# The end of a one-layer mixer and MoE kernel: residual rows summed by TensorE, second rows added by accumulating DMAs, VectorE's order written out

## The chip, the cores and the metric

The kernel runs on one core of a Trainium2 chip. The metric is device time in microseconds of one execution; of several runs the median is taken. Besides these runs one execution was recorded by the hardware profiler; all durations and starts below are from that one, in microseconds from the start of its span unless marked ns.

## The reference

One layer of a diffusion backbone over 512 latent tokens of width 1024 (and 256 context tokens, which feed only the mixer). Behind the mixer and its residual comes a mixture of experts, then one more residual and a last norm:

```python
gates = jnp.sum(jax.nn.one_hot(expert_id, N_EXPERTS, dtype=jnp.float32) * top_w[..., None], axis=1).astype(t.dtype)
y = jnp.zeros_like(t)
for e in range(N_EXPERTS):
    a = jax.nn.silu(t @ w_gate[e]) * (t @ w_up[e])
    y = y + gates[:, e:e + 1] * (a @ w_down[e])
...
xs = xs + g2x * hierarchical_moe(modulate(rms_norm(xs, norm2_w[l]), sh2x, sc2x), *moe_args)
...
return rms_norm(xs, final_norm_w)
```

Each token goes to 2 of 16 experts. `g2x` is a row of 1024 factors, the same for all tokens; `rms_norm` divides a row by the root of its mean square (plus 1e-6) and multiplies it by a row of weights. All of it is float32.

## The kernel before

The last third of the kernel works expert by expert, up to 128 tokens each. The tokens of an expert are gathered from DRAM (`xg`), transposed by TensorE, multiplied by the gate and up weights (`pg`, `pu`, line 1524), gated (`a`), transposed again (`at`, line 1542), multiplied by the down weights (`py`, line 1555). To keep float32 accuracy each factor is split in a high and a low part (`hi`, `lo`, `ah`, `al`), and a product is three products of 512 columns in a faster type. The result `y`, weighted, is scattered by GpSimd's DMA to rows of `y_d` in DRAM (line 1389). Each token has two rows there, next to each other, one for each of its experts.

The last expert (15) does not go through DRAM. Its y is multiplied by g2 as well (line 1559), split into `yh` and `yl` (lines 1585 and 1586), and brought to the token rows by products with a one-hot matrix `oht` (lines 1594 and 1595, accumulators `pz{t}{j}`: tile t, half j). The 512 tokens are four tiles t of 128. For each, the other experts' rows are loaded from `y_d` (`yv`, both rows of a token, 1 MB, line 1576, issued by SP), the two rows are added by GpSimd (line 1577), multiplied by g2 (`g2b`, line 1578) and added to the residual `xs1` (line 1579), VectorE both. Then VectorE adds the accumulators to `xs1` (line 1596). The end of a tile is the norm: ScalarE squares and sums (line 1599), VectorE makes the mean (line 1600), GpSimd raises it to -1/2 (line 1601), VectorE multiplies by it and by the final weights `fw` (line 1602), and the tile `o` is stored, by SP's queue for even t and ScalarE's for odd (line 1603). `o` has two buffers for four tiles.

The order of the instructions on each engine is decided when the program is built, by a scheduler that simulates them; it is not the order of the code where nothing forces it. `tc.add_manual_dep(b, a, behind)` forces b behind a on one engine without a semaphore; `put` does so for TensorE, behind the product that was put before. `psA` and `psB` take accumulators of one bank from pools: two for `psA` (which `py` uses), six for `psB`. `raw_tile` takes the tiles of yv from the weights' buffers.

Of the kernel before, what the change touches and what calls it, by code (L numbers as in the profile page):

```python
# [16 lines left out]
P = 128  # L17
# [203 lines left out]
def tile_kernel(ctx, tc, x, c, ctxt, c_ctx, w_mod, b_mod, norm1_w, norm2_w, w_in, w_out, hg_lb, hg_norm_w,  # L221
# [1278 lines left out]
    for t in range(NLT):  # L1500
        nc.vector.tensor_scalar(oht[:, t, :], K("iota"), 128.0 * t, tl, op0=ALU.add, op1=ALU.is_equal)

    def up(e, before):
# [34 lines left out]

    def down(e, a):
        pt = psB(f"at{e}")  # L1540
        for k in range(4):
            nc.tensor.transpose(pt[:, k * P:(k + 1) * P], a[:, k * P:(k + 1) * P], ident)  # L1542
        ah = mw2.tile([P, 4, P], F32R, tag="ah", name=f"ah{e}", bufs=2)
        al = mw2.tile([P, 4, P], F32R, tag="al", name=f"al{e}", bufs=2)
        pv = pt.rearrange("p (k t) -> p k t", k=4)
        nc.scalar.copy(ah, pv)  # L1546
        nc.vector.tensor_sub(al, pv, ah.bitcast(F32))  # L1547
        y = mw2.tile([P, D], F32, tag="y", name=f"y{e}", bufs=2)
        for j in range(2):
# [81 lines left out]
```

## Time and profile before

| | |
|---|---|
| median of 3 runs | 970.18 us (967.68 to 970.53) |
| the profiled execution | 971.5 us, span 969.7 us |
| TensorE busy | 879.4 us, 91% of the span, granted clock 0.964 on the mean |
| VectorE busy | 732.4 us, 76% |
| ScalarE, GpSimd busy | 500.8 us, 217.8 us |
| loads of `y_d` into yv | 4, of 1 MB each |

The span runs from the first to the last instruction; the execution's time has some 1.8 us around it. Busy time is an average over stages with different limits, so the shares say little about the last 30 us, in which the change lies. A line such as L1577 in a row is a line of the kernel; names of tiles stand as out<-in. A granted clock of 1.00 is TensorE's upper level, 2.4 GHz; 0.50 is 1.2 GHz.

### The profile page before, as it was taken

How to read it: one execution, taken by the hardware profiler on the slowest of the kernel's cores; microseconds unless marked ns; L12 is line 12 of the kernel's file. 1: busy time of each engine (PE TensorE's matmuls, PEld its weight loads, DVE VectorE, ACT ScalarE, POOL GpSimd, SP SyncE). 2: the span in 40 equal slices, each digit the busy share in tenths (PEclk: the TensorE clock that was granted, in tenths of full speed). 3: DMA queues.
4: the chain of work that ended last, by engine and by line, in shares of the span. 5: the costliest groups of instructions: out<-in, count | busy, mean ns of one | idle time of the engine just before them, and what ended most of it. 6: DMA issues, size and time to landing. Idle time of an engine off the chain costs nothing. (4 is left out here: it accounts for less than half of the span.)

```text
span 969.7 us, 20466 instructions
## 1 busy us (share of the span) xinstructions
PE 879.4 (91%) x8205; PEld 720.3 (74%) x8205; DVE 732.4 (76%) x1378; ACT 500.8 (52%) x958; POOL 217.8 (22%) x225
## 2 busy tenths in 40 slices
PE   3999998989989999899999989899999999999962
PEld 1678877878768887787886868758888887777741
DVE  2598589746799579964474656768899898888887
ACT  4345532454246344432432333138888887887832
POOL 2232631251135213411111110011111110110040
PEclk9999998999979999899998999999999999999995
DMA  9920350201102111047227288579999999999442
GB/s 307 313 66 13 110 205 24 69 21 35 35 23 55 35 33 47 12 144 233 63 86 255 64 269 312 181 253 387 380 363 367 366 362 378 369 377 364 176 186 87
DMA packets 115436, 180.03 MB, mean 186 GB/s; under 512 B 9863, under 2 KB 49347, under 8 KB 114824
## 3 DMA queue, kind: packets, MB, share of 16 engines
q1 hardware_dynamic: 108536, 164.28, 49.8%
q0 software_dynamic: 6048, 13.13, 3.7%
q8 instruction: 66, 1.08, 0.5%
q10 hardware_dynamic: 752, 1.25, 0.4%
q14 instruction: 34, 0.28, 0.1%
HBM read 170.31 MB, written 16.27 MB: 192 GB/s over the span
## 5 line engine op out<-in xcount | busy, mean ns | idle before, releaser
L1409 DVE TENSOR_TENSOR lo<-w,hi 128x1024 fp32r<-128x1024 f32 x184 | 216.7, 1221 | 26.6 <-ACT hi L1404 24.9
L1404 ACT CAST hi<-w 128x1024 fp32r<-128x1024 f32 x184 | 186.0, 1050 | 21.7 <-PE pu L1524 9.7
L1555 PE MATMUL py<-lo,ah 128*128 128x512 f32 x128 | 51.6, 403 | 0.8
L1555 PE MATMUL py<-hi,ah 128*128 128x512 f32 x128 | 50.5, 395 | 0.7 <-ACT ah L1546 0.7
L1555 PE MATMUL py<-hi,al 128*128 128x512 f32 x128 | 49.4, 396 | 0.3 <-DVE al L1547 0.3
L1524 PE MATMUL pg<-lo,xh 128*128 128x512 f32 x120 | 48.6, 405 | 0.0
L1524 PE MATMUL pu<-lo,xh 128*128 128x512 f32 x120 | 48.2, 401 | 0.2 <-DVE lo L1409 0.2
L1524 PE MATMUL pu<-hi,xh 128*128 128x512 f32 x120 | 47.6, 396 | 0.0
L1524 PE MATMUL pg<-hi,xh 128*128 128x512 f32 x120 | 47.5, 396 | 0.0
L1389 POOL DMA_INDIRECT y_d<-y,cl x15 | 17.6, 1174 | 132.9 <-ACT y L1557 119.7
L1524 PE MATMUL pu<-hi,xl 128*128 128x512 f32 x120 | 47.3, 394 | 0.0
L1524 PE MATMUL pg<-hi,xl 128*128 128x512 f32 x120 | 47.3, 394 | 0.0
L815 POOL TENSOR_TENSOR am<-atr,cst 128x128 f32<-128x128 f32 x32 | 17.8, 558 | 123.1 <-PE po L818 108.2
L1382 POOL DMA_INDIRECT xg<-t_d,cl x15 | 19.5, 1303 | 114.3 <-PE xt L1512 104.5
L938 DVE TENSOR_TENSOR KS<-KS,F 128x384 f32<-128x384 f32 x56 | 29.7, 569 | 3.3 <-ACT km L901 2.8
L811 DVE TENSOR_SCALAR vs<-px,bs 128x128 f32<-128x128 f32 x48 | 16.6, 345 | 19.7 <-PE px L809 19.5
L1003 PE MATMUL psm<-wm,cl 128*32 128x128 f32 x512 | 26.4, 293 | 4.8 <-DMA wm<-in_w_mod_dram 4.6
L1555 PEld LDWEIGHTS py<-lo,ah 128*128 128x128 f32 x128 | 24.0, 188 | 8.7 <-DVE lo L1409 3.4
L562 DVE SCALAR_TENSOR_TENSOR vc<-lpad,cw,vc 128x512 f32<-128x512 f32 x32 | 29.8, 931 | 0.3
L562 DVE SCALAR_TENSOR_TENSOR qc<-lpad,cw,qc 128x512 f32<-128x512 f32 x32 | 29.4, 918 | 0.4
L1555 PEld LDWEIGHTS py<-hi,ah 128*128 128x128 f32 x128 | 24.0, 188 | 6.7 <-ACT ah L1546 0.9
L1555 PEld LDWEIGHTS py<-hi,al 128*128 128x128 f32 x128 | 24.1, 188 | 6.0 <-DVE al L1547 0.8
(1058 smaller groups left out, 2725.0 us busy)
## 6 DMA issues: line engine op xcount, KB each, us to landing
w<-in_w_gate_dram SPq DMA_DIRECT2D x32, 1024.0 KB, 15.6
w<-in_w_up_dram SPq DMA_DIRECT2D x32, 1024.0 KB, 15.2
w<-in_w_down_dram SPq DMA_DIRECT2D x32, 1024.0 KB, 15.6
wm<-in_w_mod_dram SPq DMA_DIRECT2D x64, 256.0 KB, 3.9
wm<-in_w_mod_dram SPq DMA_DIRECT2D x16, 512.0 KB, 8.1
y_d<-zt POOLq DMA_DIRECT2D x8, 512.0 KB, 7.7
wor<-in_w_out_dram SPq DMA_DIRECT2D x8, 512.0 KB, 4.6
yv<-y_d SPq DMA_DIRECT2D x4, 1024.0 KB, 8.9
```

The lines of the kernel that those rows point to most:

```text
L562: nc.vector.scalar_tensor_tensor(al, s, w, al, op0=ALU.mult, op1=ALU.add)
L811: nc.vector.tensor_scalar(vs, px[:, 0:P], bs[:, d, i:i + 1], None, op0=ALU.mult)
L815: nc.gpsimd.tensor_mul(am, atr[:, t, :], K(("le", "ge")[d]))
L938: nc.vector.tensor_mul(kh, kh, tt(d, 1 - d))
L1003: nc.tensor.matmul(ps[32 * c_:32 * c_ + 32, P * j:P * j + P], cl[:, kb, :], raw[:, P * c_:P * c_ + P], start=(kb == 0), stop=(kb == KB - 1))
L1382: return nc.gpsimd.indirect_dma_start(out=dst, out_offset=None, in_=t_d[:, :], in_offset=bass.IndirectOffsetOnAxis(ap=idx, axis=0), bounds ...
L1389: i_ = nc.gpsimd.indirect_dma_start(out=y_d[:, :], out_offset=bass.IndirectOffsetOnAxis(ap=idx, axis=0), in_=src, in_offset=None, bounds_c ...
L1404: nc.scalar.copy(hi, raw)
L1409: s.append(lo_on.tensor_sub(s[1], raw, s[0].bitcast(F32)))
L1524: nc.tensor.matmul(ps, m[:, kb, :], ww[:, k, :], start=(kb == 0 and n == 0), stop=(kb == KB - 1 and n == 2))
L1555: nc.tensor.matmul(ps, m[:, k, :], ww[:, k % 2, :], start=(k == 0 and n == 0), stop=(k == 3 and n == 2))
```

## The change

It changes the end, from the last expert's second half on:

- The two rows of a token are added by VectorE for tile 0 (both rows loaded at once, as before), and for tiles 1, 2 and 3 by a DMA: SP loads the first rows, and GpSimd's queue then loads the second rows with `accum_op=ALU.add` into the same tile. GpSimd's additions are gone.
- `residuals(t, j)` puts the residual into the accumulator by a float32 product of half a tile of `xs1` with the identity matrix. For tiles 0 and 1 `xs1` already holds the other experts' rows by then, and the accumulator is the sum that is squared and multiplied; for tiles 3 and 2 it holds the residual alone, and VectorE adds the accumulator to yv.
- VectorE's order from `al` to the multiplications of tiles 3 and 2 is forced by a chain, TensorE's by `put`. The tiles end in the order 0, 1, 3, 2.
- Squares, final products and stores are done by halves of 512 columns; seven of the eight stores go by SP, the last by ScalarE. Tiles 0 and 1 write into their own yv buffers, and `o` is used for tiles 3 and 2 alone.

```diff
+    def residuals(t, j):
+        pz[t, j] = (psA if t == 1 else psB)(f"pz{t}{j}")
+        put(nc.tensor.matmul(pz[t, j], ident, xs1[:, t, halves[j]], start=True, stop=False))
...
     def down(e, a):
         pt = psB(f"at{e}")
+        if e == NE - 1:
+            chained[:] = [a_pu[0]]
+            residuals(NLT - 1, 0)
         for k in range(4):
-            nc.tensor.transpose(pt[:, k * P:(k + 1) * P], a[:, k * P:(k + 1) * P], ident)
+            tr = nc.tensor.transpose(pt[:, k * P:(k + 1) * P], a[:, k * P:(k + 1) * P], ident)
+            if e == NE - 1:
+                put(tr)
+        if e == NE - 1:
+            residuals(NLT - 1, 1)
...
             else:
-                nc.vector.scalar_tensor_tensor(y[:, cs], ps, ws0[:, e:e + 1], g2b[:, cs], op0=ALU.mult, op1=ALU.mult)
+                sums(chain, j)
+                chain.append(nc.vector.scalar_tensor_tensor(y[:, cs], ps, ws0[:, e:e + 1], g2b[:, cs],
+                                                            op0=ALU.mult, op1=ALU.mult))
...
-    for t in range(NLT):
-        yv = raw_tile(len(order) + t, [P, 2, D], f"yv{t}")
-        nc.sync.dma_start(yv, y_d[2 * t * P:2 * (t + 1) * P, :].rearrange("(p k) d -> p k d", k=2))
-        nc.gpsimd.tensor_add(yv[:, 0, :], yv[:, 0, :], yv[:, 1, :])
-        nc.vector.tensor_mul(yv[:, 0, :], yv[:, 0, :], g2b)
-        nc.vector.tensor_add(xs1[:, t, :], xs1[:, t, :], yv[:, 0, :])
-    y = down(NE - 1, a)
+    for t in (1, 0, 2, 3):
+        rows = y_d[2 * t * P:2 * (t + 1) * P, :].rearrange("(p k) d -> p k d", k=2)
+        yv = raw_tile(len(order) + len(yvs), [P, 2, D], f"yv{t}")
+        yvs[t] = yv[:, 0, :]
+        if t:
+            nc.sync.dma_start(yv[:, 0, :], rows[:, 0, :])
+            nc.gpsimd.dma_start(yv[:, 0, :], rows[:, 1, :], accum_op=ALU.add)
+        else:
+            nc.sync.dma_start(yv, rows)
+            seconds[t] = yv[:, 1, :]
+
+    def sums(chain, t):
+        if t in seconds:
+            chain.append(nc.vector.tensor_add(yvs[t], yvs[t], seconds[t]))
+        chain.append(nc.vector.tensor_mul(yvs[t], yvs[t], g2b))
+        chain.append(nc.vector.tensor_add(xs1[:, t, :], xs1[:, t, :], yvs[t]))
+
+    y, chain, mm = down(NE - 1, a)
...
+        chain.append(nc.vector.tensor_sub(yl[:, cs], y[:, cs], yh[:, cs].bitcast(F32)))
+    for t in (3, 2):
+        chain.append(nc.vector.tensor_mul(yvs[t], yvs[t], g2b))
+    for a_, b_ in zip(chain, chain[1:]):
+        tc.add_manual_dep(b_.ins, a_.ins.name, behind, reason="in this order")
...
-    for t in range(NLT):
-        xo = xs1[:, t, :]
-        for j in range(2):
-            cs = slice(512 * j, 512 * j + 512)
-            ps = psB(f"pz{t}{j}")
-            nc.tensor.matmul(ps, oht[:, t, :], yh[:, cs], start=True, stop=False)
-            nc.tensor.matmul(ps, oht[:, t, :], yl[:, cs], start=False, stop=True)
-            nc.vector.tensor_add(xs1[:, t, cs], xs1[:, t, cs], ps)
-        o = mw2.tile([P, D], F32, tag="y", name=f"o{t}", bufs=2)
-        ss = mw2.tile([P, 2], F32, tag="ss3", name=f"s3{t}", bufs=2)
-        nc.scalar.activation(o, xo, AF.Square, accum_out=ss[:, 0:1])
-        nc.vector.tensor_scalar(ss[:, 1:2], ss[:, 0:1], 1.0 / D, EPS, op0=ALU.mult, op1=ALU.add)
-        nc.gpsimd.tensor_tensor(ss[:, 1:2], ss[:, 1:2], half[:, 0:1], op=ALU.pow)
-        nc.vector.scalar_tensor_tensor(o, xo, ss[:, 1:2], fw, op0=ALU.mult, op1=ALU.mult)
-        (nc.sync, nc.scalar)[t % 2].dma_start(out[0, t * P:(t + 1) * P, :], o)
+    chained[:] = [mm]
+    turns_ = (0, 1, 3, 2)
+    for t in turns_:
+        for u in ((0, 1), (), (), (2,))[turns_.index(t)]:
+            residuals(u, 0)
+            residuals(u, 1)
+        for j, cs in enumerate(halves):
+            put(nc.tensor.matmul(pz[t, j], oht[:, t, :], yh[:, cs], start=False, stop=False))
+            put(nc.tensor.matmul(pz[t, j], oht[:, t, :], yl[:, cs], start=False, stop=True))
+        o = yvs[t] if t < 2 else mw2.tile([P, D], F32, tag="y", name=f"o{t}", bufs=2)
+        ss = mw2.tile([P, 4], F32, tag="ss3", name=f"s3{t}", bufs=NLT)
+        zs = [pz[t, j] for j in range(2)]
+        if t >= 2:
+            for j, cs in enumerate(halves):
+                nc.vector.tensor_add(yvs[t][:, cs], yvs[t][:, cs], pz[t, j])
+            zs = [yvs[t][:, cs] for cs in halves]
+        for j, (z, cs) in enumerate(zip(zs, halves)):
+            nc.scalar.activation(o[:, cs], z, AF.Square, scale=1.0 / 32.0, accum_out=ss[:, j:j + 1])
+        nc.vector.tensor_scalar(ss[:, 2:3], ss[:, 0:1], ss[:, 1:2], EPS, op0=ALU.add, op1=ALU.add)
+        nc.gpsimd.tensor_tensor(ss[:, 3:4], ss[:, 2:3], half[:, 0:1], op=ALU.pow)
+        for j, (z, cs) in enumerate(zip(zs, halves)):
+            nc.vector.scalar_tensor_tensor(o[:, cs], z, ss[:, 3:4], fw[:, cs], op0=ALU.mult, op1=ALU.mult)
+            (nc.scalar if t == turns_[-1] and j else nc.sync).dma_start(out[0, t * P:(t + 1) * P, cs], o[:, cs])
```

VectorE at the end, before, from `al` of the last expert on (y15 is its y, in two halves from py150 and py151; yv0 and yv1 are tiles 0 and 1; pz00 is the first half of tile 0):

```order
L1547 TENSOR_TENSOR al15_11233<-at15_11227,ah15_11232 128x512
L1559 SCALAR_TENSOR_TENSOR y15_11236<-py150_11237,cl_156,g2b_7492 128x512
L1578 TENSOR_TENSOR yv0_11207<-yv0_11207,g2b_7492 128x1024
L1586 TENSOR_TENSOR yl_11282<-y15_11236,yh_11281 128x512
L1579 TENSOR_TENSOR xs1_7386<-xs1_7386,yv0_11207 128x1024
L1559 SCALAR_TENSOR_TENSOR y15_11236<-py151_11259,cl_156,g2b_7492 128x512
L1578 TENSOR_TENSOR yv1_11212<-yv1_11212,g2b_7492 128x1024
L1596 TENSOR_TENSOR xs1_7386<-xs1_7386,pz00_11287 128x512
L1586 TENSOR_TENSOR yl_11282<-y15_11236,yh_11281 128x512
L1579 TENSOR_TENSOR xs1_7386<-xs1_7386,yv1_11212 128x1024
L1578 TENSOR_TENSOR yv2_11217<-yv2_11217,g2b_7492 128x1024
```

The same place after:

```order
L1563 TENSOR_TENSOR al15_11228<-at15_11218,ah15_11227 128x512
L1609 TENSOR_TENSOR yv0_11210<-yv0_11210 128x1024
L1610 TENSOR_TENSOR yv0_11210<-yv0_11210,g2b_7492 128x1024
L1611 TENSOR_TENSOR xs1_7386<-xs1_7386,yv0_11210 128x1024
L1578 SCALAR_TENSOR_TENSOR y15_11231<-py150_11232,cl_156,g2b_7492 128x512
L1610 TENSOR_TENSOR yv1_11207<-yv1_11207,g2b_7492 128x1024
L1611 TENSOR_TENSOR xs1_7386<-xs1_7386,yv1_11207 128x1024
L1578 SCALAR_TENSOR_TENSOR y15_11231<-py151_11257,cl_156,g2b_7492 128x512
L1619 TENSOR_TENSOR yl_11282<-y15_11231,yh_11281 128x512 x2
L1621 TENSOR_TENSOR yv3_11215<-yv3_11215,g2b_7492 128x1024
L1621 TENSOR_TENSOR yv2_11212<-yv2_11212,g2b_7492 128x1024
```

Tile 0's addition has come in from GpSimd. Both tiles 0 and 1 are brought into xs1 ahead of the second half of y, and both halves of y stand ahead of yl and of any work on an accumulator pz; the additions of pz to xs1 are gone.

TensorE after, behind the last `py` product; cst is the identity (of the last tile's four products here only the first two are shown):

```order
L1510 MATMUL pz00_11289<-xs1_7386,cst_70 128x512
L1510 MATMUL pz01_11291<-xs1_7386,cst_70 128x512
L1510 MATMUL pz10_11293<-xs1_7386,cst_70 128x512
L1510 MATMUL pz11_11295<-xs1_7386,cst_70 128x512
L1633 MATMUL pz00_11289<-yh_11281,oht_8639 128x512
L1634 MATMUL pz00_11289<-yl_11282,oht_8639 128x512
L1633 MATMUL pz01_11291<-yh_11281,oht_8639 128x512
L1634 MATMUL pz01_11291<-yl_11282,oht_8639 128x512
L1633 MATMUL pz10_11293<-yh_11281,oht_8639 128x512
L1634 MATMUL pz10_11293<-yl_11282,oht_8639 128x512
```

Before, the products with yh and yl stood there alone. The four identity products of tiles 0 and 1 come ahead of them; those of tile 3 stand around the transposes `at`, those of tile 2 behind tile 3's products.

GpSimd before, behind the last scatter:

```order
L1577 TENSOR_TENSOR yv0_11207<-yv0_11207 128x1024
L1577 TENSOR_TENSOR yv1_11212<-yv1_11212 128x1024
L1577 TENSOR_TENSOR yv2_11217<-yv2_11217 128x1024
L1577 TENSOR_TENSOR yv3_11222<-yv3_11222 128x1024
L1601 TENSOR_TENSOR s30_11296<-s30_11296,half_71 128x1
```

and after:

```order
L1601 DMA yv1_11207<-y_d_687 128x1024
L1601 DMA yv2_11212<-y_d_687 128x1024
L1601 DMA yv3_11215<-y_d_687 128x1024
L1645 TENSOR_TENSOR s30_11301<-s30_11301,half_71 128x1
L1645 TENSOR_TENSOR s31_11314<-s31_11314,half_71 128x1
```

Three DMAs stand where the four additions stood, in the order of tiles 1, 2, 3, and tile 3's power comes ahead of tile 2's.

## Rows read from the trace of the kernel before

**Rows 1.** Windows of the end: busy us by engine (instructions), clock, DMA share, GB/s.
```profile
930.00:938.00 8.00, 6.56 (x28) 4.93 (x29) 5.31 (x6) 1.55 (x3) 5.14 (x3) 1.00 1.01 427
938.00:941.40 3.40, 0.70 (x3) 0.21 (x2) 3.40 (x3) 0.00 (x0) 3.40 (x2) 1.00 0.35 149
...
946.00:952.00 6.00, 5.29 (x12) 3.44 (x12) 6.00 (x9) 1.31 (x4) 0.00 (x0) 0.62 0.00 0
```

**Rows 2.** Timeline of VectorE: start, us, line, form, count, idle before.
```profile
935.93 0.75 DVE L1559 SCALAR_TENSOR_TENSOR y<-py,cl,g2b 128x512 f32<-128x512 f32 x1 [2.69 <-PE py L1555]
936.60 2.06 DVE L1578 TENSOR_TENSOR yv<-yv,g2b 128x1024 f32<-128x1024 f32 x1
938.58 2.82 DVE L1586 TENSOR_TENSOR yl<-y,yh 128x512 fp32r<-128x512 f32 x1
941.33 3.37 DVE L1579 TENSOR_TENSOR xs<-xs,yv 128x1024 f32<-128x1024 f32 x1
944.62 0.74 DVE L1559 SCALAR_TENSOR_TENSOR y<-py,cl,g2b 128x512 f32<-128x512 f32 x1
945.28 1.21 DVE L1578 TENSOR_TENSOR yv<-yv,g2b 128x1024 f32<-128x1024 f32 x1
946.41 0.68 DVE L1596 TENSOR_TENSOR xs<-xs,pz 128x512 f32<-128x512 f32 x1
947.01 0.68 DVE L1586 TENSOR_TENSOR yl<-y,yh 128x512 fp32r<-128x512 f32 x1
```

**Rows 3.** Timeline of ScalarE, end.
```profile
960.50 1.06 ACT L1599 ACTIVATE o<-xs 128x1024 f32<-128x1024 f32 x1 [7.50 <-DMA out_dram<-o]
...
965.96 0.35 ACTq L1603 DMA_DIRECT2D out_dram<-o  x1
```

**Rows 4.** Timeline of GpSimd, end.
```profile
932.72 10.90 POOL L1577 TENSOR_TENSOR yv<-yv 128x1024 f32<-128x1024 f32 x4 [7.30 <-DVE lo L1409]
```

**Rows 5.** Chain that ended last, from 955: start, us, what.
```profile
957.76 2.64 DMA out_dram<-o
...
961.68 0.17 DVE s L1600
...
962.57 0.39 DVE o L1602
```

**Rows 6.** Timeline of SP's queue, end.
```profile
927.70 2.10 SPq L1576 DMA_DIRECT2D yv<-y_d  x4
```

**Rows 7.** The tile yv: its loads' time to landing.
```profile
DMA to landing us min/median/max: 4.9/8.9/10.9
```

**Rows 8.** DMA issues, whole kernel: queue, count, KB each, median us to landing.
```profile
out_dram<-o ACTq DMA_DIRECT2D x2, 512.0 KB, 2.7
...
t_d<-tt POOLq DMA_DIRECT2D x1, 512.0 KB, 3.0
...
xg<-t_d,cl POOLq DMA_INDIRECT x15, 7.5
```

**Rows 9.** Timeline of TensorE's products, end.
```profile
930.42 0.66 PE L1542 MATMUL at<-cst,a 128*128 128x128 f32 x4 [1.16 <-DVE a L1536]
931.75 0.50 PE L1555 MATMUL py<-hi,ah 128*128 128x512 f32 x1 [0.68 <-ACT ah L1546]
...
933.29 0.50 PE L1555 MATMUL py<-hi,al 128*128 128x512 f32 x1 [0.34 <-DVE al L1547]
...
937.83 0.39 PE L1555 MATMUL py<-hi,al 128*128 128x512 f32 x1
...
941.46 0.74 PE L1595 MATMUL pz<-yl,oht 128*128 128x512 f32 x2 [2.77 <-DVE yl L1586]
946.07 1.65 PE L1594 MATMUL pz<-yh,oht 128*128 128x512 f32 x3 [3.87 <-ACT yh L1585]
```

**Rows 10.** Timeline of TensorE, the first expert's float32 products.
```profile
642.58 4.45 PE L1437 MATMUL pg<-w,xg 128*128 128x512 f32 x10
```

**Rows 11.** The tile jk: squares of half a tile, ns min/median/max.
```profile
L1238 ACT ACTIVATE jk<-xs x8: 630/632/636, 591.8 to 622.6; 128x512 f32<-128x512 f32 x8
```

More of the change, by code (lines that the diff above doesn't have):

```diff
@@ L1501, in tile_kernel @@
         nc.vector.tensor_scalar(oht[:, t, :], K("iota"), 128.0 * t, tl, op0=ALU.add, op1=ALU.is_equal)
+    a_pu = [None]
+    halves = [slice(0, 512), slice(512, 1024)]
+    pz = {}
+    def residuals(t, j):
+        pz[t, j] = (psA if t == 1 else psB)(f"pz{t}{j}")
+        put(nc.tensor.matmul(pz[t, j], ident, xs1[:, t, halves[j]], start=True, stop=False))
     def up(e, before):
@@ L1523, in product @@
                     for n, (m, ww) in enumerate(((xh, hi), (xh, lo), (xl, hi))):
-                        nc.tensor.matmul(ps, m[:, kb, :], ww[:, k, :], start=(kb == 0 and n == 0),
-                                         stop=(kb == KB - 1 and n == 2))
+                        a_pu[0] = nc.tensor.matmul(ps, m[:, kb, :], ww[:, k, :], start=(kb == 0 and n == 0),
+                                                   stop=(kb == KB - 1 and n == 2))
             return ps
@@ L1546, in down @@
         nc.scalar.copy(ah, pv)
-        nc.vector.tensor_sub(al, pv, ah.bitcast(F32))
+        chain = [nc.vector.tensor_sub(al, pv, ah.bitcast(F32))]
         y = mw2.tile([P, D], F32, tag="y", name=f"y{e}", bufs=2)
@@ L1554, in down @@
                 for n, (m, ww) in enumerate(((ah, hi), (ah, lo), (al, hi))):
-                    nc.tensor.matmul(ps, m[:, k, :], ww[:, k % 2, :], start=(k == 0 and n == 0), stop=(k == 3 and n == 2))
+                    mm = nc.tensor.matmul(ps, m[:, k, :], ww[:, k % 2, :], start=(k == 0 and n == 0), stop=(k == 3 and n == 2))
+                    if e == NE - 1:
+                        tc.add_manual_dep(mm.ins, chained[-1].ins.name, behind, reason="in this order")
             if e < NE - 1:
@@ L1558, in down @@
             else:
-                nc.vector.scalar_tensor_tensor(y[:, cs], ps, ws0[:, e:e + 1], g2b[:, cs], op0=ALU.mult, op1=ALU.mult)
+                sums(chain, j)
+                chain.append(nc.vector.scalar_tensor_tensor(y[:, cs], ps, ws0[:, e:e + 1], g2b[:, cs],
+                                                            op0=ALU.mult, op1=ALU.mult))
         if e < NE - 1:
             scatter(y, ix0[:, 0, e:e + 1])
-        return y
+        return y, chain, mm
     def before(e, a):
@@ L1572, in tile_kernel @@
         a = up(e, before(e - 1, a))
-    for t in range(NLT):
-        yv = raw_tile(len(order) + t, [P, 2, D], f"yv{t}")
-        nc.sync.dma_start(yv, y_d[2 * t * P:2 * (t + 1) * P, :].rearrange("(p k) d -> p k d", k=2))
-        nc.gpsimd.tensor_add(yv[:, 0, :], yv[:, 0, :], yv[:, 1, :])
-        nc.vector.tensor_mul(yv[:, 0, :], yv[:, 0, :], g2b)
-        nc.vector.tensor_add(xs1[:, t, :], xs1[:, t, :], yv[:, 0, :])
-    y = down(NE - 1, a)
+    yvs, seconds = {}, {}
+    for t in (1, 0, 2, 3):
[14 more added lines that the diff above has]
+    y, chain, mm = down(NE - 1, a)
     yh = mw2.tile([P, D], F32R, tag="xh", name="yh", bufs=2)
@@ L1585, in tile_kernel @@
         nc.scalar.copy(yh[:, cs], y[:, cs])
-        nc.vector.tensor_sub(yl[:, cs], y[:, cs], yh[:, cs].bitcast(F32))
-    for t in range(NLT):
-        xo = xs1[:, t, :]
-        for j in range(2):
-            cs = slice(512 * j, 512 * j + 512)
-            ps = psB(f"pz{t}{j}")
-            nc.tensor.matmul(ps, oht[:, t, :], yh[:, cs], start=True, stop=False)
-            nc.tensor.matmul(ps, oht[:, t, :], yl[:, cs], start=False, stop=True)
-            nc.vector.tensor_add(xs1[:, t, cs], xs1[:, t, cs], ps)
-        o = mw2.tile([P, D], F32, tag="y", name=f"o{t}", bufs=2)
-        ss = mw2.tile([P, 2], F32, tag="ss3", name=f"s3{t}", bufs=2)
-        nc.scalar.activation(o, xo, AF.Square, accum_out=ss[:, 0:1])
-        nc.vector.tensor_scalar(ss[:, 1:2], ss[:, 0:1], 1.0 / D, EPS, op0=ALU.mult, op1=ALU.add)
-        nc.gpsimd.tensor_tensor(ss[:, 1:2], ss[:, 1:2], half[:, 0:1], op=ALU.pow)
-        nc.vector.scalar_tensor_tensor(o, xo, ss[:, 1:2], fw, op0=ALU.mult, op1=ALU.mult)
-        (nc.sync, nc.scalar)[t % 2].dma_start(out[0, t * P:(t + 1) * P, :], o)
+        chain.append(nc.vector.tensor_sub(yl[:, cs], y[:, cs], yh[:, cs].bitcast(F32)))
```

## The prediction

> **What bounds the kernel now.** The page comes first: TensorE is busy for 91% of the span (table above), so it bounds the kernel as a whole. The end is another regime, as the windows there show [rows 1]: from 938.0 on VectorE is busy for every microsecond of a window, 3.40 of 3.40 and 6.00 of 6.00, while TensorE does 0.70 of 3.40. The program up to the last `py` product (it starts at 937.83 and has streamed by about 938.2 [rows 9]) stands in the same order in both kernels, so only what comes behind it can change: 969.7 - 938.2 = 31.5 us.
>
> VectorE's own timeline [rows 2] says what these consist of. After an idle 2.69 us it starts at 935.93, and its last product ends as the last store is issued, at 965.96 [rows 3]. Three of its first five operations are stretched: 2.06, 2.82 and 3.37 us, against 1.21 for the multiplication of a whole tile and 0.68 for a half one later. They lie beside GpSimd's four additions, 10.90 us from 932.72 on [rows 4]; the excess is 0.85 + 2.14 + 2.16 = 5.15 us. The second half of y is made at 944.62, although its accumulator was full at 938.2: it stands behind them in VectorE's order. TensorE waits 2.77 and 3.87 us for it [rows 9].
>
> The chain of waits [rows 5] shows the second thing. The first output tile is stored at 957.76 and needs 2.64 us; ScalarE's third square waits for that store (its buffer is one of two) 7.50 us [rows 3]. Behind it lie, one after the other, square, mean, power on GpSimd and final product, twice. From the start of the mean to the product it takes 962.57 - 961.68 = 0.89 us. The last store, issued at 965.96 by ScalarE, takes 2.7 [rows 8], so 1.0 us of the span lies behind it.
>
> **Prices.** Starting steps of VectorE from [rows 2]: whole tile 946.41 - 945.28 = 1.13, half tile 947.01 - 946.41 = 0.60, half tile with two multipliers (y) 945.28 - 944.62 = 0.66. The means on one column I take at 0.06 (an estimate: 0.17 in [rows 5], most of it beside the next operation). ScalarE squares half a tile in 0.63 [rows 11], and some 0.8 with reading the sum (an estimate: the whole-tile square is 1.06, and the mean starts 1.18 behind its start [rows 3, 5]).
>
> **GpSimd's additions go.** VectorE gets back 5.15 us. Tile 0's addition moves onto it: +1.13.
>
> **Loads of y_d.** Before, four loads of 1 MB are issued from 927.70 [rows 6]; the first lands after 4.9 us, the last after 10.9 [rows 7], at 427 GB/s [rows 1]. 1.05 MB at that rate is 2.5 us, so 2.4 are lead. After, half a tile (tile 1, first rows) goes ahead of tile 0: 1.2 us more, so tile 1's half lands at 931.3 and tile 0 at 933.8. VectorE is free at 935.93 - 2.69 = 933.24 [rows 2], so it waits there 0.6 us; I take 934.0. A lower bound is 933.3 (the old landing, 932.6, and VectorE's being free), an upper one 935.2 (another half tile squeezed in).
>
> **Accumulating DMAs.** No trace row has one. Nearest rows: 512 KB stored by GpSimd's queue take 3.0 us, a 512 KB gather by the same queue, beside full traffic, 7.5 [rows 8]. Each is issued once its first rows have landed, about 931.3, 935.0 and 936.3. With 3.0 they land at 934.3, 938.0, 939.3, with 7.5 at 938.8, 942.5, 943.8. VectorE wants tile 1 at 938.1, tile 3 at 942.4 and tile 2 at 943.5 (below); GpSimd serves tile 2 ahead of tile 3. So the cost lies between nothing and 0.7 + 0.7 = 1.4 us. I take 0: the traffic is no gather by index, and beside it the loads run out by about 940 (the last is issued near 929 and lands 10.9 later). What waits behind a late one is the whole rest: y's second half stands behind tile 1 on VectorE, and yh, yl and all of TensorE's pz products behind that.
> The Trainium skill (Collectives: The Full Stack, "The bandwidth ceiling") says that an add in a DMA needs two source reads and so runs at half the rate of a copy. No run here shows that for a load. By it the end would be 1.3 us later than my sum, a rival below.
>
> **Identity products.** Eight, float32, 512 columns. The float32 products of the first expert are 10 records in 4.45 us, two for each product [rows 10], so 0.86 us each at full clock. pz30 lies in TensorE's wait for a (1.16 us idle before `at` [rows 9]). pz31 lies in the 0.68 it waits for ah; the 0.2 over is given back, since the fifth product then waits for al anyway (933.24 against some 932.9). The other six lie behind the last py. If the cover were gone they would cost 1.7 us. In exchange, VectorE's two whole-tile additions of xs for tiles 2 and 3 go, and for tiles 0 and 1 the half-tile additions of pz (4 x 0.60).
>
> **The walk.** VectorE from 934.0: tile 0 add, multiply, add xs to 937.4; y first half 937.4; tile 1 multiply 938.1, add 939.2; y second half 940.4, yl 941.0 and (after yh, 941.8) 941.8; tiles 3 and 2 multiplied from 942.4 to 944.7.
> TensorE from 938.2: identities of pz00, pz01 to 939.9; pz10 waits for tile 1's xs (940.4), to 941.2; pz11 needs y's second half (its bank) and ends 942.1; then products of 0.23 each: pz00 942.6, pz01 943.0, tile 1 944.0, tile 3 944.9, identities of tile 2 946.6, its products 947.6.
> ScalarE has both squares of tile 0 by 944.5, so VectorE sets the pace: mean 944.7; tile 3's first half; product of tile 0 at 945.6 (0.89 behind the mean) and 946.2; tile 3's second half 946.9; mean 947.5; tile 2's halves 947.6 and 948.2; mean of tile 3 948.8; products of tile 1 948.8 and 949.5, tile 3 950.2 and 950.8; mean of tile 2 951.4; its products 952.3 and 953.0, done 953.6. For handoffs between engines that are not counted I add 0.5 (an estimate: ten of 0.05): 954.1. The last store, 256 KB, has half of 512 KB's bytes (1.25 us at 427 GB/s): 2.7 - 0.6 = 2.1. The seven stores before it go from SP's queue some 0.7 apart, as VectorE makes them, and issuing one takes 0.35 [rows 3], so none is queued behind another. So 954.1 + 0.1 + 2.1 + 1.0 = 957.3, against 969.7: 12.4 us less. No square waits for a store any more: tiles 0 and 1 write into their own yv buffers.
> The profiled execution took 971.5 for its span of 969.7, 1.3 above the median of 970.18. Taking 12.4 from the median gives **957.8 us**.
>
> **Rivals.**
> *The adds move their bytes twice.* Then 1.57 MB more pass at 427 GB/s: the queues are busy until 940.0 + 3.7 = 943.7, tile 3 comes 1.3 late: 959.1. For it: a read and a write of the same place; against: no row.
> *The adds come one at a time and slowly,* the case on the other side. The third lands three services behind 931.3; tile 3 is wanted at 942.4. Up to 3.7 us each costs nothing; at 6 us each 6.9 is lost (964.7); at (942.4 + 12.4 - 931.3) / 3 = 7.8 us each the gain is gone; at 9 us it ends at 973.7 or so, 3.5 slower. For it: the gather's 7.5; against: gathers overlap weight loads, the quiet store needs 3.0.
> *TensorE at half clock.* Behind its wait of 3.87 us TensorE takes 1.65 us for three products, and the granted clock of that window is 0.62 [rows 1, 9]: the level of 1.2 GHz for most of it. If the six identities ran so, 1.72 each, and the rest at 0.43, tile 2's last half would be ready at 955.4, not 947.6, and VectorE wants it at 948.2: 7.2 lost, 965.0. Against: in the walk no wait of TensorE is over 0.5 us, and the clock stayed at 1.00 in the window from 938.0 to 941.4, through the wait of 2.77 us.
> *The change doesn't act:* the order given on VectorE is the shown one, so this needs a new stall that gives back all but 2.9 us; I name none but the two above.
>
> **Chances.** 0.60 for the walk (956 to 958.9), 0.20 for bytes twice (959 to 961), 0.08 for half clock (961 to 966), 0.08 for slow adds that still leave a gain (961 to 967), 0.04 for slow ones that take it all. A measurement of this kernel tells 0.3% (2.9 us) from no change; the runs shown lie within 0.3%. So faster 0.93, same 0.03, slower 0.04. The range goes down to 955.3 (tile 0 at its lower bound, no semaphore pauses, the spread of the runs) and up to 964, into half clock and slow adds.
>
> **What would show it.** In the trace after: VectorE from its tile 0 addition to the last product in about 20 us, with whole tiles at 1.2 and no 2 to 3 us rows; the first addition starting at about 934; y's second half at about 940.4; no ScalarE wait for a store; granted clock 1.00 until the last pz. Wrong would make it: the multiplication of yv1 waiting for a DMA on GpSimd's queue, the same before yv3, records of the identity products standing 0.86 us apart and not 0.43, or the last VectorE row ending past 958.

## The result and the profile after

The changed kernel takes 961.9 us (median of 17 runs, 957.52 to 967.66), the kernel before, measured beside it, 968.98 us (17 runs, 964.92 to 973.07): ratio 0.9933, 95% interval 0.9913 to 0.9953. By that ratio it is faster by 6.5 us (4.6 to 8.4), where 12.4 were forecast. The time lies inside the range, 4.1 us above the number. The gain fell short by more, 5.9 us: the number was worked out from a median of three runs, 970.18, and that of 17 is 1.2 us lower.

The profiled execution took 960.25 us for its span of 958.5. Its program up to the last `py` product stands in the same order as before but for the two identity products of tile 3, and these delay nothing: from the start of `at` to that of the last `py` product it is 935.15 - 927.73 = 7.42 us, before 7.41 [rows 9]. It ran 2.7 us earlier than in the profile before (935.15 against 937.83), as executions of one kernel scatter. The change is therefore read from there on. I call **tail** the time from the start of the last `py` product to the end of the span: before 969.7 - 937.83 = 31.87 us, after 958.5 - 935.15 = 23.35 us. The tail became 8.5 us shorter; the forecast was 31.87 - 12.4 = 19.5, so 3.9 us are missing. The tail before was read in one execution, and how much it scatters is not known; the 8.5 us lie at the upper end of what the times allow.

VectorE's timeline of the kernel after (start, us, line, form, count, idle before):

```profile
929.86 0.68 DVE L1563 TENSOR_TENSOR al<-at,ah 128x512 fp32r<-128x512 f32 x1
931.75 1.22 DVE L1609 TENSOR_TENSOR yv<-yv 128x1024 f32<-128x1024 f32 x1 [1.21 <-DMA yv<-y_d]
933.01 1.22 DVE L1610 TENSOR_TENSOR yv<-yv,g2b 128x1024 f32<-128x1024 f32 x1
934.27 1.22 DVE L1611 TENSOR_TENSOR xs<-xs,yv 128x1024 f32<-128x1024 f32 x1
935.41 0.74 DVE L1578 SCALAR_TENSOR_TENSOR y<-py,cl,g2b 128x512 f32<-128x512 f32 x1
937.21 1.22 DVE L1610 TENSOR_TENSOR yv<-yv,g2b 128x1024 f32<-128x1024 f32 x1 [1.05 <-DMA yv<-y_d]
938.47 1.22 DVE L1611 TENSOR_TENSOR xs<-xs,yv 128x1024 f32<-128x1024 f32 x1
939.61 0.74 DVE L1578 SCALAR_TENSOR_TENSOR y<-py,cl,g2b 128x512 f32<-128x512 f32 x1
...
942.35 2.36 DVE L1621 TENSOR_TENSOR yv<-yv,g2b 128x1024 f32<-128x1024 f32 x2 [0.61 <-DMA yv<-y_d]
944.93 0.21 DVE L1644 TENSOR_SCALAR s<-s 128x1 f32<-128x1 f32 x1 [0.22 <-ACT yv L1643]
945.71 0.69 DVE L1640 TENSOR_TENSOR yv<-yv,pz 128x512 f32<-128x512 f32 x1 [0.57 <-PE pz L1634]
...
953.18 1.42 DVE L1647 SCALAR_TENSOR_TENSOR o<-yv,s,fw 128x512 f32<-128x512 f32 x2 [0.66 <-POOL s L1645]
```

The rows of 2 to 3 us are gone [rows 2]: every whole tile takes 1.22. What is new are the waits, two of them, behind tile 0, for a DMA. GpSimd's timeline shows when these DMAs are issued:

```profile
929.70 1.00 POOL L1601 DMA_DIRECT2D yv<-y_d  x1 [6.98 <-DMA yv<-y_d]
933.55 0.89 POOL L1601 DMA_DIRECT2D yv<-y_d  x1 [2.85 <-DVE yv L1609]
934.91 0.86 POOL L1601 DMA_DIRECT2D yv<-y_d  x1 [0.47 <-issue]
```

The DMA issues from 920 on (count, KB each, median us from issue to landing):

```profile
yv<-y_d POOLq DMA_DIRECT2D x3, 512.0 KB, 7.4
```

These are the accumulating DMAs of tiles 1, 2 and 3. The first is issued at 929.70 and lands some 7.5 us later; VectorE, free at 936.16, goes on at 937.21. In the first 4.3 us behind that issue GpSimd's queue (q0) moved next to nothing, while the plain loads on SP's queue (q1) ran on; then the adds had the DMA engines to themselves. Queue, packets, MB and share of the 16 engines, from 929.7 to 934 and from 936 to 941:

```profile
q1 hardware_dynamic: 366, 1.56, 90.0%
q0 software_dynamic: 17, 0.07, 10.3%
...
q0 software_dynamic: 269, 0.98, 105.9%
```

The chain of waits runs through the first of them:

```profile
925.91 11.27 DMA yv<-y_d x2
...
937.21 1.24 DVE yv L1610
...
939.75 2.71 PE pz L1510 x4
```

TensorE's timeline shows its wait behind it:

```profile
927.73 0.66 PE L1554 MATMUL at<-cst,a 128*128 128x128 f32 x4 [0.31 <-DVE a L1545]
...
935.15 0.40 PE L1571 MATMUL py<-hi,al 128*128 128x512 f32 x1
935.55 1.98 PE L1510 MATMUL pz<-xs,cst 128*128 128x512 f32 x4
939.75 2.71 PE L1510 MATMUL pz<-xs,cst 128*128 128x512 f32 x4 [2.22 <-DVE xs L1611]
```

Windows (busy us and instructions by engine, clock, DMA share, GB/s) give the other half:

```profile
927.30:935.30 8.00, 7.35 (x31) 5.05 (x30) 6.72 (x7) 0.93 (x2) 2.28 (x3) 1.00 0.98 335
935.30:938.70 3.40, 2.23 (x6) 0.68 (x4) 2.31 (x4) 0.62 (x1) 0.47 (x1) 1.00 1.12 207
938.70:943.30 4.60, 3.55 (x7) 1.86 (x8) 3.90 (x5) 0.62 (x1) 0.00 (x0) 0.74 0.60 115
```

While the adds run alone (second window) the DMA engines are as busy as with the loads before (1.12 against 1.01 [rows 1]) and move 207 GB/s, not 427. Behind its wait of 2.22 us TensorE's granted clock is 0.74: four records of identity products take 2.71 us instead of 1.98. ScalarE's square, which waited 7.50 us for a store [rows 3], waits for none any more.

The last store is issued on ScalarE's queue:

```profile
954.62 0.35 ACTq L1648 DMA_DIRECT2D out_dram<-o  x1
```

From there to the end of the span it is 3.9 us, hardly other than before with a store of twice the bytes (969.7 - 965.96 = 3.7 [rows 3]); the sum had 2.1 + 1.0 = 3.1.

### The profile page after: what moved, and what is told of

Read it like the earlier page. It is cut to its first block, busy times and chain, and to the rows that moved or that the text cites. A ratio compares the mean times of both kernels' runs of the same rounds, so it can differ in the third digit from the quotient of the medians.

```text
span 958.5 us, 20502 instructions
## 1 busy us (share of the span) xinstructions
PE 883.3 (92%) x8221; PEld 722.3 (75%) x8221; DVE 726.5 (76%) x1377; ACT 501.6 (52%) x966; POOL 207.4 (22%) x224
## 5 line engine op out<-in xcount | busy, mean ns | idle before, releaser
L938 DVE TENSOR_TENSOR KS<-KS,F 128x384 f32<-128x384 f32 x56 | 32.3, 615 | 3.3 <-ACT km L901 2.8
L811 DVE TENSOR_SCALAR vs<-px,bs 128x128 f32<-128x128 f32 x48 | 16.6, 345 | 19.5 <-PE px L809 19.3
L1533 PEld LDWEIGHTS pu<-lo,xh 128*128 128x128 f32 x120 | 22.6, 188 | 7.9 <-DVE lo L1409 2.8
```

Of the source, the lines that this page charges most:

```text
L811: nc.vector.tensor_scalar(vs, px[:, 0:P], bs[:, d, i:i + 1], None, op0=ALU.mult)
L938: nc.vector.tensor_mul(kh, kh, tt(d, 1 - d))
L1533: a_pu[0] = nc.tensor.matmul(ps, m[:, kb, :], ww[:, k, :], start=(kb == 0 and n == 0), stop=(kb == KB - 1 and n == 2))
```

## The experiments

Each experiment is judged first by its tail, for the medians scatter by some us. Theory A: the accumulating DMAs move their bytes at half the rate and land late, and the missing time is VectorE's waiting for them and TensorE's lower clock behind. Theory B: the walk from product to product is longer than worked out, whatever the transfers do.

**The changed kernel once more** (no edit).

> The changed kernel once more, beside which the others of this call are read. The tail is taken from the start of the last py product to the end of the span: 31.87 us in the profiled execution before, 23.35 after. The medians differ by less (ratio 0.9933, 6.5 us) than the tails (8.5 us). If what lies ahead of the tail only scatters from execution to execution, the tail here is 23.35 within 0.5 and the ratio between 0.991 and 0.995; if the tail itself scatters (late DMAs), it differs by over 1 us.

959.51 us, ratio 0.9916 (0.9884 to 0.9948); tail 23.6 us. VectorE waited 1.14 us for tile 1, TensorE 2.30 us, the adds took 6.9 us (median). So the tail repeats within 0.3 us in these two executions, as expected, and what follows is compared with 23.35 to 23.6.

**Copies in place of adds.** The second rows overwrite the first ones, so that the first rows of tiles 1 to 3 are left out of the sum:

```diff
-            nc.gpsimd.dma_start(yv[:, 0, :], rows[:, 1, :], accum_op=ALU.add)
+            nc.gpsimd.dma_start(yv[:, 0, :], rows[:, 1, :])
```

> The three DMAs on GpSimd's queue copy the second rows over the first and don't add them, so the first rows of tiles 1 to 3 are left out of the result; bytes, queue, waits and every engine's order stay. Theory A (an accumulating load holds the DMA engines for twice its bytes): each lands some 3.5 us after its issue and not 7.4, VectorE's waits of 1.05 and 0.61 us for them go, TensorE's wait of 2.22 shrinks to about 1.2 and its clock stays up: tail 20.5 to 21.5. Theory B (the cost is GpSimd's queue and the wait for the first rows, not the adding): landings stay near 7.4 and the tail near 23.4.

957.39 us, ratio 0.9882 (0.9862 to 0.9902); tail 20.8 us, in theory A's range. VectorE at tile 1:

```profile
931.95 0.75 DVE L1578 SCALAR_TENSOR_TENSOR y<-py,cl,g2b 128x512 f32<-128x512 f32 x1
932.62 1.22 DVE L1610 TENSOR_TENSOR yv<-yv,g2b 128x1024 f32<-128x1024 f32 x1
```

The DMA issues:

```profile
yv<-y_d POOLq DMA_DIRECT2D x3, 512.0 KB, 4.6
```

A window behind the plain loads, in which copies run alone:

```profile
932.00:936.00 4.00, 2.84 (x6) 1.16 (x7) 3.97 (x6) 0.83 (x2) 0.28 (x1) 1.00 0.68 231
```

The same bytes on the same queue, without the add, land in 4.6 us instead of 6.9 to 7.4 (medians; theory A had said 3.5), tile 1's in 5.9 instead of 7.5. The copies move 231 GB/s at a share of 0.68, the adds 207 at 1.12: for the same share the adds move a little over half. Tile 1's wait is gone, TensorE's is 1.07 us, and the clock stayed at 1.00 up to 940. Of the 3.9 us that are missing, 2.6 to 2.8 hang on the add. That is theory A; about 1.3 are left for B and for what lies behind the last product.

**TensorE kept busy.** Three more identity products, whose result is not used, lie in its wait:

```diff
...
             residuals(u, 1)
+            if u == 0:
+                pz[2, 0] = psB("pz20")
+                for _ in range(3):
+                    put(nc.tensor.matmul(pz[2, 0], ident, xs1[:, 2, halves[0]], start=True, stop=True))
```

> Three more identity products of tile 2's first half, with no use, stand on TensorE between those of tile 0 and those of tile 1, 2.6 us in the wait of 2.2 for tile 1's xs. Theory A as to the clock (the wait lets it fall to half, and the products of pz00 to pz10 at 0.43 and not 0.23 hold VectorE up): granted clock 1.00 until the last pz, pz31 ready some 1.5 us sooner, VectorE's waits of 0.57 for it and 0.22 for ScalarE gone, tail 22.6. Rival (TensorE has slack there and the DMAs set the pace alone): tail 23.3 to 23.7.

960.51 us, ratio 0.9905 (0.9878 to 0.9932); tail 22.76 us, as theory A had it (22.6). TensorE's rows:

```profile
940.04 2.74 PE L1636 MATMUL pz<-xs,cst 128*128 128x512 f32 x6
942.74 1.98 PE L1511 MATMUL pz<-xs,cst 128*128 128x512 f32 x4
```

The identity products behind them take 1.98 us again, and VectorE's waits for `pz` and ScalarE are gone, while it still waits 1.37 us for tile 1's add. So the lower clock is worth 0.6 to 0.8 us of the missing time; the rest of theory A's share is the waiting for DMAs.

**VectorE adds everything,** no accumulating DMA, and tile 0 is loaded first:

```diff
-    for t in (1, 0, 2, 3):
+    for t in (0, 1, 3, 2):
...
-        if t:
-            nc.sync.dma_start(yv[:, 0, :], rows[:, 0, :])
-            nc.gpsimd.dma_start(yv[:, 0, :], rows[:, 1, :], accum_op=ALU.add)
-        else:
-            nc.sync.dma_start(yv, rows)
-            seconds[t] = yv[:, 1, :]
+        nc.sync.dma_start(yv, rows)
+        seconds[t] = yv[:, 1, :]
...
+        chain.append(nc.vector.tensor_add(yvs[t], yvs[t], seconds[t]))
```

> No accumulating DMA: SP loads both rows of all four tiles, in the order 0, 1, 3, 2, and VectorE adds them, three more additions of 1.2 us. Theory A: tile 0 is there when VectorE is free (1.2 us gained), the waits of 1.66 go, 3.7 are added: tail 24.0 to 24.8, so the accumulating DMAs are worth about 1 us and not 3.7. If the adds in the DMAs were free, as the prediction took them, the difference would be 3 us or more: tail over 26.

960.42 us, ratio 0.9909 (0.989 to 0.9928); tail 22.65 us. The expectation was missed by over a microsecond: three additions of 1.22 us more on VectorE, and the tail is shorter by 0.7 to 1.0. From 930.96 to the last tile's power VectorE works without a wait, each addition in the place of a wait; its rows around tile 1:

```profile
934.61 0.74 DVE L1578 SCALAR_TENSOR_TENSOR y<-py,cl,g2b 128x512 f32<-128x512 f32 x1
935.27 1.22 DVE L1605 TENSOR_TENSOR yv<-yv 128x1024 f32<-128x1024 f32 x1
```

Against this kernel the three accumulating DMAs thus bring nothing. Part of that is the order of the loads: with tile 0 first, VectorE starts on it 0.60 us behind the start of `al` (930.36), not 1.89; order and adds were not tried apart. The medians (960.42 and 959.51 beside the same runs of before) don't tell the two apart.

**GpSimd adds** tiles 1, 3 and 2, from rows loaded whole and in the order 0, 1, 3, 2 as in the kernel above:

```diff
...
-            nc.gpsimd.dma_start(yv[:, 0, :], rows[:, 1, :], accum_op=ALU.add)
+            nc.gpsimd.tensor_add(yv[:, 0, :], yv[:, 0, :], yv[:, 1, :])
```

> The changed kernel, but GpSimd adds the second rows of tiles 1, 3 and 2 as it did before, from rows loaded by SP in the order 0, 1, 3, 2; all orders of the other engines stay. If the contention of GpSimd's additions with VectorE is what the change removed (5.15 us for four), about 4 us of it come back beside VectorE's work on tiles 0 and 1: against the variant in which VectorE adds (tail 22.65, 3.7 of it those additions) the tail is 23.5 to 25, with rows of 2 us and more on VectorE. If the contention hides under other waits, it is below 22.

964.79 us, ratio 0.9945 (0.9919 to 0.9971); tail 26.29 us, worse than expected. VectorE's timeline:

```profile
933.63 3.31 DVE L1610 TENSOR_TENSOR xs<-xs,yv 128x1024 f32<-128x1024 f32 x1
...
937.52 2.71 DVE L1609 TENSOR_TENSOR yv<-yv,g2b 128x1024 f32<-128x1024 f32 x1
940.27 3.25 DVE L1610 TENSOR_TENSOR xs<-xs,yv 128x1024 f32<-128x1024 f32 x1
```

GpSimd's timeline, and TensorE's behind its wait for tile 1:

```profile
933.10 9.33 POOL L1601 TENSOR_TENSOR yv<-yv 128x1024 f32<-128x1024 f32 x3 [9.73 <-DVE yv L1608]
...
943.58 3.47 PE L1510 MATMUL pz<-xs,cst 128*128 128x512 f32 x4 [4.59 <-DVE xs L1610]
```

The stretched rows are back, 5.6 us over 3 x 1.22 (3.31 + 2.71 + 3.25 - 3.66), for as long as GpSimd adds. This is the term "GpSimd's additions go". Against the kernel in which VectorE adds all, with the same loads, the tail is 3.6 us longer, although VectorE is spared three additions of 1.22 us. Part of that is TensorE's lower clock behind its wait of 4.59 us: four records of identity products take 3.47 us and not 1.98.

**The kernel before with its first two output tiles in their own buffers:**

```diff
...
-        o = mw2.tile([P, D], F32, tag="y", name=f"o{t}", bufs=2)
-        ss = mw2.tile([P, 2], F32, tag="ss3", name=f"s3{t}", bufs=2)
+        o = yvs[t] if t < 2 else mw2.tile([P, D], F32, tag="y", name=f"o{t}", bufs=2)
+        ss = mw2.tile([P, 2], F32, tag="ss3", name=f"s3{t}", bufs=NLT)
```

> One part alone, on the kernel before: tiles 0 and 1 end in their own yv buffers, so no square waits for a store. ScalarE's wait of 7.50 us goes. Theory: the path then goes through VectorE's last addition (960.0 in the profile before), square, mean, power and product, and the end comes some 2.4 us sooner: tail 29.5 (31.87 before). Rival: the wait was covered, tail within 0.5 of 31.87.

969.49 us against 969.96, ratio 0.9994 (0.9965 to 1.0022); tail 28.69 us, 3.2 shorter than before, so the wait was not covered. The wait for the store became one for VectorE:

```profile
957.27 1.06 ACT L1601 ACTIVATE o<-xs 128x1024 f32<-128x1024 f32 x1 [2.44 <-DVE xs L1598]
```

The median shows nothing of it (its interval reaches from 3.4 us faster to 2.1 slower). Its last `py` product started at 940.51, and its `py` products took 7.09 us from the first to the last, against 6.08 before, so the gain is better counted from the start of `al` ahead of them, before and here:

```profile
932.55 0.69 DVE L1547 TENSOR_TENSOR al<-at,ah 128x512 fp32r<-128x512 f32 x1
...
934.22 0.68 DVE L1547 TENSOR_TENSOR al<-at,ah 128x512 fp32r<-128x512 f32 x1
```

To the end of the span it is 37.15 us from the one and 34.98 from the other, 2.2 less, where 2.4 were expected. Whether this part alone is worth that in the time stays open.

**The kernel before with accumulating DMAs** for all four tiles:

```diff
...
-        nc.sync.dma_start(yv, y_d[2 * t * P:2 * (t + 1) * P, :].rearrange("(p k) d -> p k d", k=2))
-        nc.gpsimd.tensor_add(yv[:, 0, :], yv[:, 0, :], yv[:, 1, :])
+        nc.sync.dma_start(yv[:, 0, :], rows[:, 0, :])
+        nc.gpsimd.dma_start(yv[:, 0, :], rows[:, 1, :], accum_op=ALU.add)
```

> One part alone, on the kernel before: GpSimd's additions of all four tiles become accumulating DMAs; the rest of the code stays, but the scheduler puts both halves of y ahead of the tiles on VectorE. Contention (5.15 us) goes and the store wait (2.4) stays; the adds come about 12 us after the first load's issue (7.4 each) and VectorE waits for the first of them: tail 26.5 to 28.5. If accumulating DMAs were as cheap as predicted, 25.5 or less.

970.04 us, ratio 1.0008 (0.998 to 1.0036); tail 32.67 us: no gain, where a tail of 26.5 to 28.5 was expected. The DMA issues:

```profile
yv<-y_d POOLq DMA_DIRECT2D x4, 512.0 KB, 8.5
```

TensorE's timeline:

```profile
953.01 0.80 PE L1595 MATMUL pz<-yh,oht 128*128 128x512 f32 x1 [7.71 <-DVE xs L1597]
```

ScalarE's timeline:

```profile
963.55 1.06 ACT L1600 ACTIVATE o<-xs 128x1024 f32<-128x1024 f32 x1 [6.43 <-DMA out_dram<-o]
```

The stretched rows are gone here too, and yet four adds that land after 8.5 us, with the store that ScalarE waits for, hold the end where it was. VectorE's order is another one too, so this is not the adds alone. One cause taken away shows only the next one.

**Tile 1 plain,** VectorE adds tiles 0 and 1, tiles 3 and 2 come by accumulating DMAs:

```diff
-        if t:
+        if t > 1:
```

(with the loads in the order 0, 1, 3, 2)

> Between the changed kernel and the variant without accumulating DMAs: tiles 0 and 1 are loaded whole, first, and added by VectorE, tiles 3 and 2 are added by DMA, in the order in which VectorE takes them. Theory A: only the add of tile 1 and the late start of tile 0 cost in the changed kernel; VectorE starts 1.2 us sooner, adds 1.2, waits about 0.7 for tile 3: tail 21.3 to 22.2, better than either (23.35 and 22.65). Rival: the two adds, side by side, land later than 8 us after their issue and the tail is 22.6 or more.

961.45 us, ratio 0.9913 (0.9884 to 0.9942); tail 22.83 us, which is the rival's, though not for its reason. GpSimd's timeline:

```profile
937.50 2.00 POOL L1601 DMA_DIRECT2D yv<-y_d  x2 [12.16 <-DMA yv<-y_d]
```

VectorE's timeline:

```profile
943.92 1.23 DVE L1621 TENSOR_TENSOR yv<-yv,g2b 128x1024 f32<-128x1024 f32 x1 [0.75 <-DMA yv<-y_d]
946.44 1.23 DVE L1621 TENSOR_TENSOR yv<-yv,g2b 128x1024 f32<-128x1024 f32 x1 [1.30 <-DMA yv<-y_d]
```

Both first halves stand last on SP's queue and land together, so both adds start together, and only at 937.50. The first lands 6.4 us later, not over 8: the lateness moved from tile 1 to tiles 3 and 2.

**No identity products;** VectorE adds the accumulators to the residual for all tiles:

```diff
-        put(nc.tensor.matmul(pz[t, j], ident, xs1[:, t, halves[j]], start=True, stop=False))
+        return
...
+        for j, cs in enumerate(halves):
+            nc.vector.tensor_add(xs1[:, t, cs], xs1[:, t, cs], pz[t, j])
+        zs = [xs1[:, t, cs] for cs in halves]
```

> The changed kernel without its identity products: VectorE adds the accumulators to the residual rows for all four tiles, and the rows of tiles 3 and 2 to the residual before. That is four half rows of 0.7 us for tiles 0 and 1 and two whole rows of 1.2 us for tiles 3 and 2 more on VectorE, about 5.2 us. If VectorE sets the end of the changed kernel (my theory after the runs so far), the part of it that falls in VectorE's waits for the late second rows is lost and the rest is added: from the start of the last expert's last product to the end 26.5 to 28.5 us, against 23.4 to 23.6 in the changed kernel. If the transfers and TensorE set it (rival), most of the 5.2 us lies in waits: 23.5 to 25.5 us. TensorE has 8 records of 0.4 us less between its last py product and the first pz one.

964.37 us, ratio 0.9942 (0.9914 to 0.9971); tail 25.92 us, between the two expectations. But the tail flatters it here: its `py` products took 7.33 us from first to last, against 6.09 in the changed kernel, at a granted clock of 0.78 in that window:

```profile
928.90:936.60 7.70, 7.46 (x24) 5.30 (x24) 5.87 (x6) 0.11 (x1) 2.75 (x3) 0.78 1.02 323
```

VectorE's side doesn't wait for that. Its last row ahead of tile 0 is `al`:

```profile
929.75 0.68 DVE L1562 TENSOR_TENSOR al<-at,ah 128x512 fp32r<-128x512 f32 x1
```

From there it is 962.2 - 929.75 = 32.45 us to the end, against 958.5 - 929.86 = 28.64 in the changed kernel: the identity products are worth 3.8 us, of 5.2 us of VectorE's work that they take over.

**One accumulating DMA alone,** that of tile 2, its first rows loaded second:

```diff
-    for t in (1, 0, 2, 3):
+    for t in (0, 2, 1, 3):
...
-        if t:
+        if t == 2:
...
+        if t == 3:
+            chain.append(nc.vector.tensor_add(yvs[t], yvs[t], seconds[t]))
```

> One accumulating DMA alone, that of the tile that is needed last (tile 2), its first rows loaded second; the other three tiles come with both rows, and VectorE adds them. In the kernel in which VectorE adds all four it worked without a wait, with 22.65 us from the start of the last py product to the end; this takes one add of 1.22 us away. If the accumulating DMA has time enough there (needed some 6 us after it lands, if it lands within 9 us of its issue) and nothing else becomes the bound, 21.2 to 21.9 us, and the time 8 to 10 us under the kernel before. If it slows the plain loads beside it as much as it saves (rival), VectorE waits for yv of tile 1 or 3, and it is 22.5 us or more.

959.22 us, ratio 0.9882 (0.9854 to 0.991) against 0.9933 and 0.9916 of the changed kernel; tail 21.7 us, as expected. GpSimd's timeline:

```profile
934.06 1.01 POOL L1601 DMA_DIRECT2D yv<-y_d  x1 [9.79 <-DMA yv<-y_d]
```

VectorE's timeline:

```profile
943.27 2.36 DVE L1623 TENSOR_TENSOR yv<-yv,g2b 128x1024 f32<-128x1024 f32 x2
```

TensorE's timeline:

```profile
940.11 1.98 PE L1510 MATMUL pz<-xs,cst 128*128 128x512 f32 x4 [1.30 <-DVE xs L1611]
```

The add is issued at 934.06, lands 6.7 us later and is wanted at about 944.4. VectorE never waits for a DMA, and the clock holds. In the tail this is 1.7 to 1.9 us better than the changed kernel and 0.95 better than VectorE adding all; the intervals of the times nearly touch or overlap (0.9854 to 0.991 beside 0.9913 to 0.9953 and 0.9884 to 0.9948), so the time itself doesn't settle it.

**Tiles 3 and 2 whole again** in square, product and store:

```diff
-        for j, (z, cs) in enumerate(zip(zs, halves)):
+        parts = list(zip(zs, halves)) if t < 2 else [(yvs[t], slice(0, D))]
...
+        for j, (z, cs) in enumerate(parts):
```

> The changed kernel, with the squares, the last product and the store of tiles 3 and 2 whole instead of in halves. For the last tile the product takes 1.2 us whole before its store starts instead of the second half's start at 0.7 us behind the first, and the store of 512 KB 2.7 us instead of 2.1 us for 256 KB on two queues; the square of the whole row starts with the second half's add instead of the first's, 0.6 us later, and takes about 1.1 us instead of two of 0.63. So 0.6 to 1.3 us later: 24.0 to 24.9 us from the start of the last py product to the end, against 23.4 to 23.6. If halves are worth nothing (rival): 23.3 to 23.8.

A single time, 966.86 us, says nothing at this scatter; tail 23.88 us (span 965.1), just below the range expected and just above the rival's. The halves of the last tiles are worth some 0.3 to 0.5 us, about what the tail repeats to, so it isn't shown that they gain anything.

The tails, from the profiled execution of each kernel (us):

| kernel | span | start of the last `py` | tail |
|---|---|---|---|
| before | 969.7 | 937.83 | 31.87 |
| changed | 958.5 | 935.15 | 23.35 |
| changed, once more | 957.0 | 933.40 | 23.6 |
| copies in place of adds | 952.4 | 931.60 | 20.8 |
| TensorE kept busy | 960.5 | 937.74 | 22.76 |
| VectorE adds everything | 958.3 | 935.65 | 22.65 |
| GpSimd adds | 962.1 | 935.81 | 26.29 |
| before, own buffers | 969.2 | 940.51 | 28.69 |
| before, accumulating DMAs | 973.1 | 940.43 | 32.67 |
| tile 1 plain | 960.6 | 937.77 | 22.83 |
| no identity products | 962.2 | 936.28 | 25.92 |
| one accumulating DMA | 958.4 | 936.70 | 21.7 |
| tiles 3 and 2 whole | 965.1 | 941.22 | 23.88 |

## Why the prediction was right, and where its size was off

That the time lies in the range is owed to the range's width: 961.9 is above the band of the walk (956 to 958.9) and that of bytes twice (959 to 961). The scatter was taken too small as well: 0.3% (2.9 us) from three runs, where 17 runs of the kernel before spread over 8 us.

*GpSimd's additions go:* right. No row is stretched after; with GpSimd adding again, 5.6 us of stretch come back.

*Tile 0 at 934.0:* 931.75 + 2.7 = 934.4; off by 0.4. The first half tile landed 4.7 us after its issue (925.00 to 929.70), not 3.6: no sooner than the whole tile of before.

*Accumulating DMAs, "I take 0":* this step failed. They took 6.9 to 7.4 us (medians), the upper of the two bounds (7.5), and were issued 1.1 to 1.3 us later than worked out, the first since its first half landed late. I had taken the store of a quiet moment for the nearer row; the loads beside them and the add itself spoke for the other. Beside the plain loads the adds' queue moved 0.07 MB in 4.3 us, and behind them the adds moved at half the rate. Why it stood still is not shown: with tile 1 plain, when the loads were over, it still moved only 0.05 MB in its first 2.5 us. The sign of being wrong came as named: yv1's multiplication waited 1.05 us for GpSimd's queue, yv3's 0.61. With it fell "no wait of TensorE is over 0.5 us": it waited 2.22 us, and the clock fell behind that (with copies it still waited 1.07, so the walk alone breaks this, too). The price, put between nothing and 1.4 us, was 2.6 to 2.8: that much of the 3.9 us copies in place of the adds win back, some 0.6 to 0.8 of it by the clock. The rival "the adds move their bytes twice" had the mechanism (207 GB/s at a share of 1.12, copies 231 at 0.68) and half its price: it charged 1.3 us at tile 3 alone, where tile 1, issued first and wanted first, is late as well, with all that stands behind it. The Trainium skill (Collectives: The Full Stack, "The bandwidth ceiling") has the adding step of a ring of ranks at half the rate of its copying step, because the add needs two source reads. The rates here, 207 GB/s of adds against 427 of plain loads, agree with a half; the share of reads was not measured.

*Slow adds that take all the gain:* no; their times from issue to landing overlap, so three land within 13 us of the first's issue.

*TensorE at half clock:* in part, 0.74 for 4.6 us, not to the end.

*Identity products hidden:* right. pz30 and pz31 delay nothing, and without all eight 3.8 us are lost.

*The walk:* its order was right, the pace of VectorE a little short. A whole-tile step that reads the result of the one before takes 1.26 us (931.75, 933.01, 934.27), not the 1.13 of rows that follow unrelated ones. This, tile 0 and handoffs make up some 0.5 of the 1.3 us that stay missing with copies; their shares were read from the profile and not tried one by one.

*No square waits for a store, last store 2.1 us:* both as forecast, yet the smaller store gained nothing: from its issue to the end of the span it is 3.9 us (with copies too, 948.53 to 952.4), where the sum had 3.1. These 0.8 us are the rest of the 1.3; what fills the time behind the landing is not shown.

*A reading:* the wait of 2.77 us [rows 9] was for the first half's yl, not for y's second half; the sum doesn't use it.

## What to carry to other kernels

A transfer that is to take work from an engine has its own time from issue to landing, and it is worth something only where the consumer comes later than that: here one add for the tile that is needed last helped (tail 21.7 us against 22.65 with VectorE adding all), three did not (23.35). When two rows bound an unknown price from both sides, take the one whose surroundings (traffic beside it, queue, read and write of one place) are those of the new place. Compare kernels from an event that all of them share to the end of the span; whole runs scatter by more than such an edit is worth, and several causes that lie behind one another show their worth only together.

## What the runs showed of the hardware that was not expected

- An accumulating DMA of 512 KB on GpSimd's queue landed after 6.4 to 8.5 us (medians of the kernels here), the same DMA as a copy after 4.6. In the first 4.3 us behind its issue, while SP's queue moved 1.56 MB, GpSimd's moved 0.07; alone, the adds moved 207 GB/s.
- The end of the span came 3.7 us behind the issue of a last store of 512 KB and 3.9 us behind that of one of 256 KB.
- In the changed kernel TensorE's granted clock fell behind a wait of 2.22 us (0.74); with waits of 1.07 us (second rows copied) and 1.30 us (one accumulating DMA) it stayed at 1.00. In the kernel before it stayed at 1.00 in the window that ends with the wait of 2.77 us, and was 0.62 behind the later one of 3.87 us [rows 1, 9].
- Two of the four kernels without identity products ahead of `py` ran part of these products at a lower clock (7.09 and 7.33 us instead of 6.1), none of the nine with them. This was not followed up.
